# Keys side by side, runs of 32 in the first softmax pass, and other places for TensorE's turns, in a two-layer streaming encoder

## The chip, the cores and the metric

The kernel runs on one core of a Trainium2 chip. The time is the device time of one execution in microseconds, the median of several. The core has TensorE (matrix products; a transposition is also a product, with an identity matrix), VectorE (DVE in the rows), ScalarE (ACT), GpSimd (POOL) and SyncE (SP, which here only issues transfers). Each has an instruction queue of its own, worked off in order; ScalarE also issues transfers (ACTq in the rows). 16 DMA engines move the data.

## The reference

One inference step of an encoder with two layers (DEPTH = 2), width 1024. Two groups of requests share the weights: one prompt of 256 tokens, and 8 decode requests of 16 new tokens, each with a cache of 512 past tokens. A layer is, cut to what matters here:

```python
proj = x @ w_in          # FoX q, k, v, forget gates | Diff q, k, v | gates A, B
# branch A: 8 heads of 64, logits plus a decay summed along the keys
s = einsum('bqhd,bkhd->bhqk', qb, k) * scale + cq - c_k
p = softmax(where(mask, s, -1e30)); oa = einsum('bhqk,bkhd->bqhd', p, v)
# branch B: 4 heads, two softmaxes of 64 wide queries and keys each
s = einsum('bqhcd,bkhcd->bchqk', qb, k) * scale - slopes * dist
p = softmax(where(mask, s, -1e30)); a = p[:, 0] - lam * p[:, 1]
merged = sigmoid(gA) * (oa @ w_ba) + sigmoid(gB) * (ob @ w_bb)
x = LN(ALPHA * x + merged @ w_o)
x = LN(ALPHA * x + (silu(x @ w_g) * (x @ w_u)) @ w_d + sigmoid(x @ w_pg) * (p_ple @ w_pp))
```

The keys and values of a decode request are the cache's 512 and its own 16, 528 in all. Both branches have a cache, so there are 2 x 8 decode streams in a layer and 32 in the run. Outputs are x of both groups and the new keys, values and forget gates.

## The kernel before

All products are made in fp32 quality: a weight tile is split into a high part (`wh`, a cast on ScalarE) and a low part (`wl`, a subtraction on VectorE), an activation likewise (`xh`, `xl`), and three products are summed in PSUM: high times high (L163), low times high (L164), high times low (L165), in `three`. The 384 tokens (256 of the prompt, 128 of the decodes) are three tiles of 128. A weight comes in units of 512 KB (`wr`); a body of a projection runs through eight steps in its input dimension, K tiles of 128, each one call of `three`.

The first half of a layer is one list of such bodies, `work`, for `w_in` and the two branch weights, and the attention is laid between its pieces by hand: `work.fill(us)` emits K tiles until so many (estimated) microseconds are out, then an attention step is emitted, then more K tiles. So the order on each engine is the order in which the program text emits the instructions; nothing reorders them. Smaller steps are handed to a planner: `plan(after, go, pe)` puts a step into a list with a due time on the same estimated clock, and `steps()` runs it between two K tiles when the clock has come to it. A step that holds work for TensorE itself (`pe` true: the transposition of new keys for the output, `out_t`; the decay's sums and turns, `decay_2`, `decay_3`, `sums`; the norm of the prompt's heads; the rows of the per-layer embedding, `ple_rows`) is called a turn here and may stand only behind the first or the third K tile of a body (n = 0 or 2), one to a body.

The attention's decode streams go in a pipeline, one `it` after the other: transposition of the stream's probabilities (`probs`), scores of the next (`scores`), its softmax (`soft`), products of this one with its values (`values`), normalisation of the next (`norm`). Four prompt heads a branch are items of the same kind and stand among its eight streams.

The keys of a stream come as `kr`, [128 partitions, 8, 256]; VectorE transposes them in 32 x 32 blocks into `KT` (L685, two instructions), and GpSimd copies the 16 own keys beside them (L691). A partition of `KT` holds, for each of eight head slices, 8 rows of 34 floats: row c, place r is key 8r + c, and two places in each row take own keys. A score product (L708) takes 264 +- 8 keys of a half `i` in the keys' order, which in `KT` is one float of each row in turn. The 32 score matmuls of a stream are eight tiles of 64 x 32 on the array, twice (d), in the two passes of an fp32 product.

`soft` reads the scores from PSUM: one VectorE instruction for each half of the keys (L717) adds the bias, writes the result to `pm` and keeps the minimum; L720 joins the two minima and ScalarE takes the exponential (L722). For requests 0 to 3 the 16 own keys stand first in `pm`, else last, and the biases (`rt`, `dbs`) are laid out to match.

## Time and profile before

| | |
|---|---|
| median of 3 runs | 1377.43 us (1376.71 to 1377.6) |
| profiled execution | 1381.31 us |
| its span | 1379.5 us |
| granted clock of TensorE, mean | 0.993 |
| TensorE busy | 1329.3 us, 96% |
| VectorE, ScalarE, GpSimd busy | 730.8, 532.2, 173.9 us |
| moved by DMA | 235.12 MB, 170 GB/s |

The span begins with the first instruction and ends with the last, and the profiled execution's time has 1.8 us around it. Busy time is the union of an engine's instructions. TensorE's weight loads (PEld) run beside its products. The lines named are those of the kernel before. The attention of the first layer lies between 87 and 354 us, that of the second between 771 and 981 us.

### The profile page before, as it was taken

How to read it: one execution, taken by the hardware profiler on the slowest of the kernel's cores; microseconds unless marked ns; L12 is line 12 of the kernel's file. 1: busy time of each engine (PE TensorE's matmuls, PEld its weight loads, DVE VectorE, ACT ScalarE, POOL GpSimd, SP SyncE). 2: the span in 40 equal slices, each digit the busy share in tenths (PEclk: the TensorE clock that was granted, in tenths of full speed). 3: DMA queues.
4: the chain of work that ended last, by engine and by line, in shares of the span. 5: the costliest groups of instructions: out<-in, count | busy, mean ns of one | idle time of the engine just before them, and what ended most of it. 6: DMA issues, size and time to landing. Idle time of an engine off the chain costs nothing. (4 is left out here: it accounts for less than half of the span.)

```text
span 1379.5 us, 22688 instructions
## 1 busy us (share of the span) xinstructions
PE 1329.3 (96%) x9102; PEld 1173.8 (85%) x9102; DVE 730.8 (53%) x1290; ACT 532.2 (39%) x1015; POOL 173.9 (13%) x370
## 2 busy tenths in 40 slices
PE   6989999999999999999999999999899999999997
PEld 6978787778889999999998777877788899999996
DVE  3555556656635444444565556666566444344355
ACT  3434544343433333333333335444444333233241
POOL 0042222213200000000014112211132000000001
PEclk9999999999999999999999999999999999999999
DMA  8869897835334344344669697887352444444351
GB/s 249 238 171 266 238 260 204 240 108 193 125 122 123 122 123 138 121 126 153 192 193 255 170 262 241 224 239 211 103 203 89 121 123 130 130 127 131 123 184 46
DMA packets 179673, 235.12 MB, mean 170 GB/s; under 512 B 13392, under 2 KB 143984, under 8 KB 179568
## 3 DMA queue, kind: packets, MB, share of 16 engines
q1 hardware_dynamic: 136272, 190.65, 46.7%
q10 hardware_dynamic: 43296, 43.03, 11.0%
q8 instruction: 71, 1.16, 0.4%
q14 instruction: 34, 0.28, 0.1%
HBM read 223.90 MB, written 9.75 MB: 169 GB/s over the span
## 5 line engine op out<-in xcount | busy, mean ns | idle before, releaser
L163 PE MATMUL tp<-xh,wh 128*128 128x384 f32 x1216 | 419.8, 345 | 0.0
L165 PE MATMUL tp<-xh,wl 128*128 128x384 f32 x1216 | 410.7, 338 | 0.6 <-DVE wl L362 0.6
L164 PE MATMUL tp<-xl,wh 128*128 128x384 f32 x1216 | 408.6, 336 | 0.0
L145 DVE TENSOR_TENSOR wl<-wr,wh 128x1024 fp32r<-128x1024 f32 x158 | 196.2, 1242 | 236.8 <-ACT wh L144 236.5
L144 ACT CAST wh<-wr 128x1024 fp32r<-128x1024 f32 x162 | 170.0, 1049 | 251.8 <-PE zz L165 137.6
L163 PEld LDWEIGHTS tp<-xh,wh 128*128 128x128 f32 x1216 | 228.5, 188 | 8.9 <-issue 7.1
L164 PEld LDWEIGHTS tp<-xl,wh 128*128 128x128 f32 x1216 | 229.2, 188 | 0.8
L165 PEld LDWEIGHTS tp<-xh,wl 128*128 128x128 f32 x1216 | 228.0, 188 | 1.5 <-DVE wl L362 1.2
L362 DVE TENSOR_TENSOR wl<-wr,wh 128x1024 fp32r<-128x1024 f32 (+1 forms) x88 | 115.3, 1310 | 54.4 <-ACT wh L359 54.1
L359 ACT CAST wh<-wr 128x1024 fp32r<-128x1024 f32 (+1 forms) x88 | 92.5, 1051 | 37.6 <-PE tp L164 15.9
L1088 POOL TENSOR_TENSOR st<-st,mhalf 128x1 f32<-128x1 f32 x8 | 12.2, 1523 | 646.4 <-DVE st L1087 646.4
L163 PE MATMUL zz<-wh,pT 128*128 128x512 f32 x216 | 84.8, 393 | 0.0
L165 PE MATMUL zz<-wh,ev 128*128 128x512 f32 x216 | 84.6, 392 | 0.0
L164 PE MATMUL zz<-wl,pT 128*128 128x512 f32 x216 | 84.4, 391 | 0.0
L685 DVE STREAM_TRANSPOSE KT<-kr 128x1024 f32<-128x1024 f32 x64 | 76.5, 1225 | 0.0
L691 POOL COPY KT<-s 32x32 f32<-32x32 f32 x256 | 70.1, 274 | 12.5 <-POOL zp L731 0.2
L708 PE MATMUL S<-KT,s 64*32 64x272 f32 (+1 forms) x1024 | 70.3, 658 | 0.0
L163 PE MATMUL tp<-wh,xh 128*128 128x256 f32 (+1 forms) x192 | 57.7, 300 | 6.9 <-DVE s L262 3.6
L164 PE MATMUL tp<-wl,xh 128*128 128x256 f32 (+1 forms) x192 | 56.3, 293 | 3.7 <-DVE wl L362 3.7
L165 PE MATMUL tp<-wh,xl 128*128 128x256 f32 (+1 forms) x192 | 55.8, 291 | 0.0
L722 ACT ACTIVATE pm<-pm,nmx 128x528 f32<-128x528 f32 x32 | 23.6, 737 | 76.7 <-DVE nmx L720 76.7
L163 PE MATMUL tp<-s,wh 128*128 128x384 f32 x128 | 46.6, 364 | 3.3 <-DVE s L323 1.8
(230 smaller groups left out, 1919.4 us busy)
## 6 DMA issues: line engine op xcount, KB each, us to landing
wr<-in_w_in ACTq DMA_DIRECT2D x72, 512.0 KB
wr<-in_w_ffn_gate SPq DMA_DIRECT2D x44, 512.0 KB
wr<-in_w_ffn_up SPq DMA_DIRECT2D x44, 512.0 KB
wr<-in_w_ffn_down SPq DMA_DIRECT2D x44, 512.0 KB
vr<-in_cache_fox_v SPq DMA_DIRECT2D x16, 1024.0 KB
vr<-in_cache_diff_v SPq DMA_DIRECT2D x16, 1024.0 KB
kr<-in_cache_fox_k SPq DMA_DIRECT2D x16, 512.0 KB
kr<-in_cache_fox_k SPq DMA_DIRECT2D x32, 256.0 KB
```

What stands on the lines that cost most here:

```text
L144: S.copy(hi, raw)
L145: (eng or V).tensor_tensor(lo, raw, hi.bitcast(F32), ALU.subtract)
L163: T.matmul(ps, lhsT=ah, rhs=bh, start=start, stop=False)
L164: T.matmul(ps, lhsT=ah, rhs=bl, start=False, stop=False)
L165: T.matmul(ps, lhsT=al, rhs=bh, start=False, stop=stop)
L359: S.copy(hi, self.raws[len(self.parts)])
L362: return lambda n=len(self.parts) - 1: V.tensor_tensor(lo, self.raws[n], hi.bitcast(F32), ALU.subtract)
L685: V.transpose(kt[:, 4 * c4:4 * c4 + 4], kr[:, 4 * c4:4 * c4 + 4, :].rearrange("p c (n a) -> p c n a", n=8))
L691: G.tensor_copy(KT[r].rearrange("p (j n) c t -> p j n t c", j=2)[:, :, jj, new:new + 2], own.rearrange("p j (t c) -> p j t c", c=8))
L708: T.matmul(s[32 * g:32 * g + 32, i, 0:n[i]], lhsT=qr[r, 2 * g + d, self.b, :], rhs=KT[r, 2 * g + d, :, k0[i]:k0[i] + n[i] // 8].rearrange( ...
L722: S.activation(pm, pm, AF.Exp, bias=nmx, scale=-1.0, accum_out=self.su)
L1088: G.tensor_tensor(st[:, 7:8], st[:, 6:7], mhalf[:, 0:1], ALU.pow)
```

## The change

The places of keys in `KT` become contiguous: a head slice is a row of 272 floats, the half's 256 cached keys and then the 16 own keys, and a score product reads them one beside the other. To have blocks of 32 in that order the key loads take row 64c + 32i + r of the cache (c of 8, half i, r of 32) instead of eight neighbouring rows to a partition. Scores so come in the order of the halves, (i, c, r); the first pass of the softmax, three VectorE instructions instead of two, writes them back in the order of the keys (c, i, r) in runs of 32, and the own keys at the end. One reduction joins three minima. The biases lose their second layout.

The second part is on turns: `plan` now takes the K tiles of a body behind which a turn may stand, (2,) for nearly all, (0,) for the turns of the input and (2, 6) for the rows of the per-layer embedding, which are also due 1 us sooner. A body may take a second turn behind its seventh K tile. In the turns of the input (`turn_x`) all eight transpositions stand ahead of the two splits, for which `split_g` is divided in two. Lastly the first item's normalisation is emitted after 2.5 of the 4.5 us of K tiles that follow its softmax, not ahead of them.

```diff
@@ -71,7 +71,7 @@
     sm[:, SEQ::NQ] = 0.0
     c["c_scan"] = sm
     slopes = 2.0 ** (-8.0 * np.arange(1, H_B + 1) / H_B)
-    kpos = np.concatenate([PAST + jj, np.arange(PAST), PAST + jj])
+    kpos = np.arange(NK)
     qpos = PAST + q
     ds = -8.0 * slopes[row_block() // 2][:, None] * np.abs(qpos[:, None] - kpos[None, :])
     ds = np.where(kpos[None, :] // CHUNK <= qpos[:, None] // CHUNK, ds, -BIG)
...
@@ -171,10 +171,14 @@
             three(ps, hi[:, k % 4, m * P:(m + 1) * P], lo[:, k % 4, m * P:(m + 1) * P],
                   ah[:, k, :], al[:, k, :], k == 0, k == n - 1)
 
-    def split_g(src, tt, hi_t, lo_t, g, n, t=None):
-        t = tp() if t is None else t
+    def turn_g(src, g, n, t):
         for j in range(n):
             T.transpose(t[:, j * P:(j + 1) * P], src[:, (g + j) * P:(g + j + 1) * P], ident)
+
+    def split_g(src, tt, hi_t, lo_t, g, n, t=None):
+        if t is None:
+            t = tp()
+            turn_g(src, g, n, t)
         tv = t[:, :n * P].rearrange("p (k t) -> p k t", k=n)
         hs = hi_t[:, g:g + n, tt * P:(tt + 1) * P]
         S.copy(hs, tv)
...
@@ -288,7 +292,7 @@
                     (S.copy if j % 2 else V.tensor_copy)(kT[:, j, :], ps[:, :NT])
                     if j == 3:
                         for tt in range(3):
-                            plan(2.5 + 4.0 * tt, out_t(tt), True)
+                            plan(2.5 + 4.0 * tt, out_t(tt), (2,))
                 return go
             return [(cols(w_in, D, col + 256 * i), [fm_body(m, out(2 * i + m)) for m in range(2)]) for i in range(2)]
 
...
@@ -326,7 +330,8 @@
 
         plans, clock, due = [], [0.0], [0]
 
-        def plan(after, go, pe=False):
+        def plan(after, go, pe=()):
+
 
             t = clock[0] + after
             i = len(plans)
...
@@ -383,7 +388,8 @@
                                 due[0] += 1
                             was = u
                             clock[0] += cost
-                            while plans and plans[0][0] <= clock[0] and not (plans[0][2] and (n not in (0, 2) or pe)):
+                            pe = pe and n != 6
+                            while plans and plans[0][0] <= clock[0] and not (plans[0][2] and (n not in plans[0][2] or pe)):
                                 pe = pe or plans[0][2]
                                 plans.pop(0)[1]()
                             yield gi, cost
...
@@ -652,10 +658,10 @@
             if g < 2 * NB:
                 K = caches[g // NB][0][g % NB]
                 kr = raws[g] = at.tile([P, 8, 256], F32, name="kr")
-                nc.sync.dma_start(out=kr[32:96], in_=K[:, 0:256].rearrange("(r c) f -> r c f", c=8))
+                nc.sync.dma_start(out=kr[32:96], in_=K[:, 0:256].rearrange("(c p) f -> p c f", c=8))
                 for i in range(2):
                     nc.sync.dma_start(out=kr[part(i, 1):part(i, 1) + 32],
-                                      in_=K[NHF * i:NHF * (i + 1), 256:512].rearrange("(r c) f -> r c f", c=8))
+                                      in_=K[:, 256:512].rearrange("(c i r) f -> i r c f", c=8, i=2)[i])
 
         def load_v(g):
             if g < 2 * NB:
...
@@ -664,11 +670,10 @@
 
         def load_rt(b):
             if b < NB:
-                old, new = (NQ, 0) if b < 4 else (0, PAST)
                 rt = rts[b] = at.tile([P, NK], F32, name="rt")
-                nc.sync.dma_start(out=rt[:, old:old + PAST],
+                nc.sync.dma_start(out=rt[:, 0:PAST],
                                   in_=raw_ap(r8_d[l], b * 8 * PAST, [[PAST, 8], [0, NQ], [1, PAST]]))
-                G.tensor_copy(rt[:, new:new + NQ], nbm[:, b, :])
+                G.tensor_copy(rt[:, PAST:NK], nbm[:, b, :])
 
         def turn_k(g):
 
...
@@ -676,10 +681,9 @@
                 return lambda: None
             st, b = (fx, df)[g // NB], g % NB
             ib = b // 4
-            old, new = (2, 0) if ib == 0 else (0, 32)
-            KT = KTs[g] = at.tile([P, 8, 8, 34], F32, name="KT", bufs=1)
+            KT = KTs[g] = at.tile([P, 8, NHN], F32, name="KT", bufs=1)
             kr = raws.pop(g)
-            kt = KT[:, :, :, old:old + 32].rearrange("p n c r -> p c n r")
+            kt = KT[:, :, 0:NHF].rearrange("p n (c r) -> p c n r", c=8)
 
             def turn(c4):
                 V.transpose(kt[:, 4 * c4:4 * c4 + 4], kr[:, 4 * c4:4 * c4 + 4, :].rearrange("p c (n a) -> p c n a", n=8))
...
@@ -687,9 +691,8 @@
             turn(0)
             for x, jj in ((x, jj) for x in range(2) for jj in range(4)):
                 r = slice(part(ib, x), part(ib, x) + 32)
-                own = st["kv"][0][32 * jj:32 * jj + 32, 2 * x:2 * x + 2, SEQ + NQ * b:SEQ + NQ * b + NQ]
-                G.tensor_copy(KT[r].rearrange("p (j n) c t -> p j n t c", j=2)[:, :, jj, new:new + 2],
-                              own.rearrange("p j (t c) -> p j t c", c=8))
+                G.tensor_copy(KT[r].rearrange("p (j n) t -> p j n t", j=2)[:, :, jj, NHF:NHN],
+                              st["kv"][0][32 * jj:32 * jj + 32, 2 * x:2 * x + 2, SEQ + NQ * b:SEQ + NQ * b + NQ])
             return lambda: turn(1)
 
         class Stream:
...
@@ -701,23 +704,27 @@
             def scores(self):
                 KT, qr, ib = KTs.pop(self.g), self.st["qr"], self.b // 4
                 s = self.s = sp.tile([P, 2, 512], F32, name="S", bufs=2)
-                n = self.n = [NHN if i == ib else NHF for i in range(2)]
-                k0 = [2 if i != ib and ib == 0 else 0 for i in range(2)]
+                n = [NHN if i == ib else NHF for i in range(2)]
                 for d, i, g in ((d, i, g) for d in range(2) for i in range(2) for g in range(4)):
                     r = slice(64 * i, 64 * i + 64)
                     T.matmul(s[32 * g:32 * g + 32, i, 0:n[i]], lhsT=qr[r, 2 * g + d, self.b, :],
-                             rhs=KT[r, 2 * g + d, :, k0[i]:k0[i] + n[i] // 8].rearrange("p c t -> p t c"), start=d == 0, stop=d == 1, skip_group_check=True)
+                             rhs=KT[r, 2 * g + d, 0:n[i]], start=d == 0, stop=d == 1, skip_group_check=True)
 
             def soft(self):
-                n, bias = self.n, self.bias()
+                bias = self.bias()
                 pm = self.pm = at.tile([P, 768], F32, name="pm")[:, 0:NK]
-                nm = sm.tile([P, 2], F32, name="nm2")
-                for i in range(2):
-                    h = slice(n[0] * i, n[0] * i + n[i])
-                    V.tensor_tensor_reduce(out=pm[:, h], in0=self.s[:, i, 0:n[i]], in1=bias[:, h], scale=-0.125,
-                                           scalar=3e38, op0=ALU.add, op1=ALU.min, accum_out=nm[:, i:i + 1])
+                nm = sm.tile([P, 3], F32, name="nm3")
+
+                def part_of(t, i):
+                    return t[:, 0:PAST].rearrange("p (c i r) -> p i c r", c=8, i=2)[:, i]
+
+                for i in range(3):
+                    src, b, out = ((self.s[:, i, 0:NHF].rearrange("p (c r) -> p c r", c=8), part_of(bias, i), part_of(pm, i))
+                                   if i < 2 else (self.s[:, self.b // 4, NHF:NHN], bias[:, PAST:NK], pm[:, PAST:NK]))
+                    V.tensor_tensor_reduce(out=out, in0=src, in1=b, scale=-0.125, scalar=3e38, op0=ALU.add,
+                                           op1=ALU.min, accum_out=nm[:, i:i + 1])
                 nmx = sm.tile([P, 1], F32, name="nmx")
-                V.tensor_tensor(nmx, nm[:, 0:1], nm[:, 1:2], ALU.min)
+                V.tensor_reduce(nmx, nm, mybir.AxisListType.X, ALU.min)
                 self.su = sm.tile([P, 1], F32, name="su1")
                 S.activation(pm, pm, AF.Exp, bias=nmx, scale=-1.0, accum_out=self.su)
 
...
@@ -727,14 +734,12 @@
                 if self.st is df:
                     V.tensor_tensor(rs, rs, coef, ALU.mult)
                 V.tensor_scalar(self.pm, self.pm, rs, None, ALU.mult)
-                new = 0 if self.b < 4 else PAST
-                G.tensor_copy(zp[:, 112:128], self.pm[:, new:new + NQ])
+                G.tensor_copy(zp[:, 112:128], self.pm[:, PAST:NK])
 
             def probs(self):
-                old = NQ if self.b < 4 else 0
                 t = sp.tile([P, 512], F32, name="pt")
                 for c in range(4):
-                    T.transpose(by_block(t[:, c * P:(c + 1) * P]), self.pm[:, old + P * c:old + P * (c + 1)], ident)
+                    T.transpose(by_block(t[:, c * P:(c + 1) * P]), self.pm[:, P * c:P * (c + 1)], ident)
                 tn = self.s[:, 1, 384:512]
                 T.transpose(by_block(tn), zp[:, 112 - NQ * self.b:240 - NQ * self.b], ident)
                 self.pT = at.tile([P, 512], F32, name="pT")
...
@@ -866,7 +871,7 @@
                 ple_load(0)
                 ple_load(1)
                 for tt in range(3):
-                    plan(2.0 + 2.0 * tt, lambda tt=tt: ple_rows(tt), True)
+                    plan(1.0 + 2.0 * tt, lambda tt=tt: ple_rows(tt), (2, 6))
 
         def ple_rows(tt):
             split_g(ple[tt], tt, ple["t"][:, 0], ple["t"][:, 1], 0, 2)
...
@@ -911,10 +916,12 @@
                 def turn_x(tt):
                     t = sp.tile([P, 2, 512], F32, name="S", bufs=2)
                     for g in range(2):
+                        turn_g(x0[:, tt, :], 4 * g, 4, t[:, g, :])
+                    for g in range(2):
                         split_g(x0[:, tt, :], tt, xh, xl, 4 * g, 4, t[:, g, :])
 
                 for tt in (1, 2):
-                    plan(0.3 + 2.9 * (tt - 1), lambda tt=tt: turn_x(tt), True)
+                    plan(0.3 + 2.9 * (tt - 1), lambda tt=tt: turn_x(tt), (0,))
             for _ in range(2):
                 work.split()
             plan(2.4, work.split)
...
@@ -923,15 +930,15 @@
             diag, causal, comb, compm, dbs = [K_[n] for n in ("diag", "causal", "comb", "comp", "dbs")]
             plan(6.0, lambda: load_k(0))
             plan(9.0, decay_1)
-            plan(10.0, decay_2, True)
+            plan(10.0, decay_2, (2,))
             plan(13.0, lambda: load_v(0))
-            plan(14.0, decay_3, True)
+            plan(14.0, decay_3, (2,))
             plan(17.0, lambda: query_slot(fx))
             plan(22.0, lambda: load_k(1))
             plan(30.0, lambda: load_v(1))
             plan(18.5, log_gates)
             plan(21.0, lambdas)
-            plan(23.5, sums, True)
+            plan(23.5, sums, (2,))
             work.fill(upto=2)
             work.fill(upto=4)
             plan(2.5, lambda: late.append(turn_k(0)))
...
@@ -944,8 +951,9 @@
             work.fill(1.0)
             its[0].scores()
             its[0].soft()
+            work.fill(2.5)
             its[0].norm()
-            work.fill(4.5)
+            work.fill(2.0)
             ends, norms, loads = [], [], []
             for i, it in enumerate(its):
                 nx = its[i + 1] if i + 1 < len(its) else None
```

On TensorE the first key turn, that of `s_156` (the new keys, transposed with `c_ident` into `tp`) among the products of a projection; before:

```order
L163 MATMUL tp<-xh,wh 128x384
L164 MATMUL tp<-xl,wh 128x384
L165 MATMUL tp<-xh,wl 128x384
L277 MATMUL tp<-c_ident,s_156 128x128 x4
L163 MATMUL tp<-xh,wh 128x384
L164 MATMUL tp<-xl,wh 128x384
L165 MATMUL tp<-xh,wl 128x384
L163 MATMUL tp<-xh,wh 128x384
L164 MATMUL tp<-xl,wh 128x384
L165 MATMUL tp<-xh,wl 128x384
```

and now:

```order
L163 MATMUL tp<-xh,wh 128x384
L164 MATMUL tp<-xl,wh 128x384
L165 MATMUL tp<-xh,wl 128x384
L163 MATMUL tp<-xh,wh 128x384
L164 MATMUL tp<-xl,wh 128x384
L165 MATMUL tp<-xh,wl 128x384
L163 MATMUL tp<-xh,wh 128x384
L164 MATMUL tp<-xl,wh 128x384
L165 MATMUL tp<-xh,wl 128x384
L281 MATMUL tp<-c_ident,s_156 128x128 x4
L163 MATMUL tp<-xh,wh 128x384
```

It has moved behind two more K tiles of the same body, six products; the other eleven key turns, and those of the decay and the sums, move by as much.

On VectorE the first normalisation of a layer (`rs` is the reciprocal of the sums `su`, `pm` the probabilities, `s_757` a tile of new values that is copied out of `tp`; the reductions are named ISA); before:

```order
L520 ISA nm 128x1
L551 RECIPROCAL rs_798<-su_785 128x4
L555 TENSOR_SCALAR pm<-pm,rs_798 128x128
L555 TENSOR_SCALAR pm<-pm,rs_798 128x256
L555 TENSOR_SCALAR pm<-pm,rs_798 128x128
L555 TENSOR_SCALAR pm<-pm,rs_798 128x256
L262 COPY s_757<-tp 128x256
L577 COPY pT<-S 128x384
L717 ISA pm,nm_877<-S,rt 128x272
L717 ISA nm_877 128x1
L717 ISA pm,nm_877<-S,rt 128x256
L717 ISA nm_877 128x1
```

and now:

```order
L526 ISA nm 128x1
L266 COPY s_757<-tp 128x256
L557 RECIPROCAL rs_823<-su_785 128x4
L561 TENSOR_SCALAR pm<-pm,rs_823 128x128
L561 TENSOR_SCALAR pm<-pm,rs_823 128x256
L561 TENSOR_SCALAR pm<-pm,rs_823 128x128
L561 TENSOR_SCALAR pm<-pm,rs_823 128x256
L583 COPY pT<-S 128x384
L724 ISA pm,nm_877<-S,rt 128x8x32
L724 ISA nm_877 128x1
L724 ISA pm,nm_877<-S,rt 128x8x32
L724 ISA nm_877 128x1
```

The copy of `s_757` stands ahead of the reciprocal and its four multiplications, and the reductions of a stream's softmax are three, two of 8 x 32 columns and one of 16.

On SyncE, which issues transfers in this order, the loads at the end of the attention (`wr` is a unit of weights, `ev` a tile of the embedding rows `p_prompt` and `p_sample`, `vr` cached values); before:

```order
L663 DMA vr<-in_cache_diff_v 128x4x512 x2
L138 DMA wr<-in_w_branch_diff 128x4x256 x2
L859 DMA ev<-in_p_prompt 128x256
L138 DMA wr<-in_w_branch_diff 128x4x256 x2
L859 DMA ev<-in_p_prompt 128x256
L859 DMA ev<-in_p_sample 128x256
L138 DMA wr<-in_w_out 128x1024 x2
```

and now:

```order
L669 DMA vr<-in_cache_diff_v 128x4x512 x2
L138 DMA wr<-in_w_branch_diff 128x4x256 x3
L864 DMA ev<-in_p_prompt 128x256
L138 DMA wr<-in_w_branch_diff 128x4x256
L864 DMA ev<-in_p_prompt 128x256
L864 DMA ev<-in_p_sample 128x256
L138 DMA wr<-in_w_out 128x1024 x2
```

The first embedding rows go out behind a third unit of `w_branch_diff` instead of behind the second.

## Rows read from the trace of the kernel before

**Rows 1.** The page's first part: busy us and share of each engine.

```profile
PE 1329.3 (96%) x9102; PEld 1173.8 (85%) x9102; DVE 730.8 (53%) x1290; ACT 532.2 (39%) x1015; POOL 173.9 (13%) x370
```

**Rows 2.** Groups by line: instruction, count | busy us, mean ns | idle before.

```profile
L685 DVE STREAM_TRANSPOSE KT<-kr 128x1024 f32<-128x1024 f32 x64 | 76.5, 1225 | 0.0
...
L708 PE MATMUL S<-KT,s 64*32 64x272 f32 x512 | 69.9, 673 | 0.0
...
L754 PE MATMUL o<-vr,pT 128*32 128x128 f32 x1024 | 34.6, 276 | 1.7 <-ACT pT L741 1.7
L754 PEld LDWEIGHTS o<-vr,pT 128*32 128x32 f32 x1024 | 26.0, 109 | 22.3 <-issue 7.7 <-ACT pN L743 6.6 <-ACT wh L359 5.8
...
L520 DVE CUSTOM_DVE_ANT_0 pm<-S,z 128x128 f32<-128x128 f32 x16 | 4.6, 289 | 10.9 <-PE S L538 10.9
```

**Rows 3.** Timeline of the first decode stream: start, length in us, instruction.

```profile
98.06 0.59 ACT L741 COPY pT<-pt 128x512 f32<-128x512 f32 x1 [3.70 <-DVE s L262]
...
98.06 2.17 PE L708 MATMUL S<-KT,s 64*32 64x272 f32 x32
...
98.54 0.17 PEld L708 LDWEIGHTS S<-KT,s 64*32 64x32 f32 x8 [0.30 <-issue]
...
99.03 0.17 PEld L708 LDWEIGHTS S<-KT,s 64*32 64x32 f32 x8 [0.32 <-issue]
...
100.16 1.08 PE L754 MATMUL o<-vr,pT 128*32 128x128 f32 x32
```

**Rows 4.** Timeline of the last decode stream, TensorE alone.

```profile
969.97 2.25 PE L708 MATMUL S<-KT,s 64*32 64x256 f32 x32
972.15 1.08 PE L754 MATMUL o<-vr,pT 128*32 128x128 f32 x32
```

**Rows 5.** Timeline behind a Fox prompt head.

```profile
86.99 2.20 PE L708 MATMUL S<-KT,s 64*32 64x272 f32 x32
...
87.61 0.56 DVE L577 COPY pT<-S 128x384 f32<-128x384 f32 x1 [1.88 <-ACT pT L576]
```

**Rows 6.** Waits of TensorE: us in total, times, longest.

```profile
PE tp L277 <- ACT s L300: 11.7, 12, 1.0
...
PE tp L164 <- DVE wl L362: 3.7, 3, 1.8
PE tp L163 <- DVE s L262: 3.6, 2, 2.2
...
PE S L177 <- DVE xl L181: 2.8, 2, 1.4
PE tp L177 <- ACT s L315: 2.3, 2, 1.2
...
PE tp L448 <- PE tp L165: 0.7, 2, 0.3
PE tp L457 <- DVE lg L264: 0.6, 2, 0.3
```

**Rows 7.** Timeline at one key turn.

```profile
152.19 0.34 PE L165 MATMUL tp<-xh,wl 128*128 128x384 f32 x1
...
152.72 0.34 PE L165 MATMUL tp<-xh,wl 128*128 128x384 f32 x1
...
154.07 0.66 PE L277 MATMUL tp<-c_ident,s 128*128 128x128 f32 x4 [1.00 <-ACT s L300]
```

**Rows 8.** Timeline at the first normalisation.

```profile
84.39 1.01 DVE L555 TENSOR_SCALAR pm<-pm,rs 128x128 f32<-128x128 f32 x4
...
86.24 0.82 PE L560 MATMUL S<-c_ident,pm 128*128 128x128 f32 x6
```

**Rows 9.** Windows: stretch, busy us of each engine, clock, DMA share, GB/s.

```profile
87.00:90.00 3.00, 3.00 (x41) 1.48 (x42) 1.14 (x4) 0.48 (x1) 0.00 (x0) 0.50 0.02 5
98.06:354.00 255.94, 248.15 (x2285) 204.86 (x2285) 154.88 (x351) 114.50 (x287) 54.21 (x147) 0.99 0.76 218
780.00:800.00 20.00, 20.00 (x196) 17.30 (x197) 10.54 (x30) 8.95 (x26) 2.31 (x10) 1.00 1.08 265
```

More of the change, by code (lines that the diff above doesn't have):

```diff
@@ L123, in constants @@
         K_["comp"] = cload("c_comp", [P, 2])
-        K_["dbs"] = cload("c_dbs", [P, NK + NQ])
+        K_["dbs"] = cload("c_dbs", [P, NK])
     mhalf = const.tile([P, 8], F32, name="mhalf")
@@ L778, in bias @@
             def bias(self):
-                return dbs[:, 0:NK] if self.b < 4 else dbs[:, NQ:NK + NQ]
+                return dbs
             def finish(self, todo):
@@ L990, in layer @@
                     plan(0.5, diff_prompt_scale)
-                    plan(4.0, lambda: diff_prompt_norm(0), True)
-                    plan(9.0, lambda: diff_prompt_norm(1), True)
+                    plan(4.0, lambda: diff_prompt_norm(0), (2,))
+                    plan(9.0, lambda: diff_prompt_norm(1), (2,))
                 if nx:
```

## The prediction

> **What bounds the kernel now.** I read the page's busy line first: TensorE works through 96% of the span and no other engine through more than 53% [rows 1]. So a microsecond taken from TensorE's own row of work, or from its idle time, shortens the run, and one taken elsewhere does not, unless TensorE waits for it. Next I read the groups by line, each tile shape apart, for what TensorE does at a rate below its usual one: the scores of the decode streams (L708) and the products with the values (L754) are both 1024 matmuls, in 32 streams of 32, and a score takes 673 ns where a product takes 276 [rows 2]. The timeline of one stream shows the rounds in which these go [rows 3], and the last stream's two rows show the same pace as the first's [rows 4]. Then the waits, for what TensorE stands idle for [rows 6], and last the load on VectorE and on the DMA engines in the attention stage [rows 9], which the change touches too.
>
> The profiled execution took 1381.31 us (span 1379.5 us), 3.9 us above the median of 1377.43. I sum against 1381.31 and take the same 3.9 us off at the end.
>
> **A: keys side by side (-32 us).** Before, one score matmul reads keys that lie 34 floats, 136 bytes, apart. The weight loads of the rounds start at 98.06 (with the first matmul), 98.54 and 99.03, so a round of eight matmuls, which lie on different pieces of the array, takes 0.485 us [rows 3]. With 256 or 272 keys, 264 in the mean, that is 1.84 ns per key; the 32 matmuls of a stream are four rounds, the two passes of the fp32 product counted. The product with the values reads its 128 columns side by side, and its rounds, of four, are as far apart as one weight load is long, 109 ns [rows 2]: 0.85 ns per column. (Eight such rounds make the stream's 1.08 us: 7 x 0.109 + 0.276 = 1.04 [rows 2, 3].) A round of 272 contiguous keys is then 0.231 us, of 256 keys 0.218; I take 0.225. What a matmul takes beyond its round is 276 - 109 = 167 ns for the contiguous one [rows 2]; the score's 673 - 485 = 188 ns is nearly the same, so it is a fixed tail. From the first score to the first product of the stream there are four rounds and one tail: 4 x 0.485 + 0.19 = 2.13 us by this, and 2.10 and 2.18 us by the rows of the first and the last stream [rows 3, 4]. After the change: 4 x 0.225 + 0.17 = 1.07, and I put 0.03 on top for the hand-over, which makes 1.10.
>
> Something else then decides in some streams: the product needs the transposed probabilities. ScalarE's copy of them ends 0.59 us after the first score [rows 3], in good time for 1.10. Where a Fox prompt head stands ahead of the scores, VectorE makes the second of two copies and ends at 88.17, 1.18 us after the first score at 86.99 [rows 5]. There are eight such places, four to a layer; I count 1.23 us for them. The sum: 24 x (2.13 - 1.10) = 24.7 and 8 x (2.13 - 1.23) = 7.2, together 32 us. The bounds: nothing, if the stride isn't what makes the round slow; 39 us, if the tail goes too (32 x (2.13 - 0.90) = 39). I take 32, since the nearest row, the product with the values, has rounds and a tail both.
>
> [...]
>
> What A adds lies on VectorE: three reductions instead of two for a softmax, in runs of 32 keys. The smallest reduction shown, 128 columns, takes 289 ns [rows 2]; the new one has 16 columns, so I bound it between 0 and 289 ns, and the two in runs between no change and twice their 0.44 us, if short runs cost what a stride cost TensorE. VectorE is busy for 154.88 of 255.94 us there [rows 9], 61%, and the next to need the probabilities is the transposition a whole stream later, some 14 us; so 0 on the path, with up to 1 us per stream late in what stands behind it on VectorE, the low halves of the weights (term G). POOL's own-key copies and the bias without its copied columns have no one waiting, as POOL is busy for 54 of 256 us [rows 9].
>
> **B: twelve key turns behind the third K tile (-12.2 us).** At each TensorE waits for ScalarE's copy of the keys, 11.7 us in 12 times [rows 6]. In the timeline the last product of the first K tile starts at 152.72 and the turn at 154.07: 1.35 us, against 0.17 between products inside a tile, so 1.18 us is lost. A K tile takes 0.53 us (152.19 to 152.72) [rows 7]. The order puts two more K tiles, 1.06 us, ahead of each turn, so 0.12 us of the wait is left: 12 x 1.06 = 12.7, less 0.5 for a start that is never as neat: 12.2. Bounds: 9 (where ScalarE's copy itself is late) to 14.
>
> **C: all eight transposes before a split (-3.2 us).** TensorE waits for VectorE's first low half before it may turn the second half, 2.8 us in two times [rows 6]; with the restart of 0.18 each (1.18 - 1.00 in B), 3.2. The splits are then late by the second half's turns, half a microsecond, for a product that stands one or two K tiles on: 0 to +1.
>
> **D: the first normalisation is issued later (-1.6 us).** TensorE waits 3.6 us in two times for a copy on VectorE (L262) that stands behind four multiplications [rows 6]; these run 84.39 to 85.40 [rows 8]. The copy now stands ahead of them, but the transposition of the same probabilities, which went at 86.24 [rows 8], needs their end; it can move up to 85.45 and no further. So 0.8 us per layer, not 1.8.
>
> **E: the small turns of decay and sums (-2.0 us).** 0.7 + 0.6 us in four waits [rows 6], with four restarts of 0.18. Two K tiles cover each.
>
> **F: the turns of the per-layer embedding rows (0).** Now two of three stand behind the last product, with waits of 2.3 us in two times [rows 6] and one behind them for the low half. After, they stand among the products, but SP issues the first row's load behind one more weight load, which may make the first turn wait as long. Bounds -3 to +3; I take 0.
>
> **G: what is late next (+2 us).** TensorE comes to its weights about 1 us sooner in each stream. It already waits 3.7 us in three times for a low half (L362) on VectorE [rows 6]. I let this grow by half, +2; bounds 0 to +16, half of A, which is the second rival.
>
> Sum: -32 - 12.2 - 3.2 - 1.6 - 2.0 + 2 = -49.0. 1381.31 - 49.0 = 1332.3, and against the median 1377.43 - 49.0 = **1328 us**.
>
> **Rivals.**
> *The array sets the pace (1360 us).* If eight matmuls side by side are slow because they share the array's input or the PSUM, contiguous keys change nothing, A is 0 and 17 us of the other terms are left: 1377.4 - 17 = 1360. For it: the score's shape is the only one with a height of 64 and four heads in a row. [...]
>
> *Half of A is handed back (1344 us).* The stream's other engines keep their pace: ScalarE's and VectorE's halves of the weights come late, or the products wait for the probabilities in all streams and not in eight. Then 16 of 32 us return: 1328 + 16 = 1344. For it: VectorE gets longer by up to 1 us a stream. Against it: it is idle in 39% of the stage, and the schedule issues the halves ahead of their use.
>
> *Slower: the loads of the keys (1392 us).* A partition's eight rows of keys now lie 64 rows, 128 KB, apart in memory, where they were neighbours, 2 KB apart. A stream has 512 x 512 floats of keys, 1.05 MB; 16 streams in 255.94 us are 66 GB/s of 218, 30% of the bytes, and of the DMA engines' share of 0.76 that is 0.23 [rows 9]. The densest stretch shows 1.08 [rows 9]; 0.76 + 0.23(f - 1) reaches it where the packets take f = 2.4 times as long, and from there TensorE waits for keys. At f = 2.7 the share would be 1.15, 6.6% above, and over the two layers' 466 us of streams (98 to 354, and 771 to 981) that is +31 us; A is hidden by it, and 17 us remain: 1377.4 + 31 - 17 = 1392. Against it: the packets stay 1 KB, the transposition of keys has never waited for its load (idle 0.0) [rows 2], and the loads of the values already jump as far, 128 rows.
>
> **How the numbers follow.** The forecast has 0.75, half of A handed back 0.14, the array's pace 0.07, the key loads 0.04. The forecast's own range: the terms' good ends (A 39, B 14, F -3, G 0) give 1377.4 - (39 + 14 + 3.2 + 1.6 + 2.0 + 3) = 1315; the bad ends that may come together (B 9, F +3, G +5) give 1328 + 3 + 3 + 3 = 1337. To hold 8 in 10 it takes in the second rival with a margin: 1315 to 1347. A measurement of this kernel can tell 0.2%, 2.8 us, from no change. Forecast and first two rivals are all faster: 0.96; of the key loads' 0.04 a quarter lies near f = 2.4 and about cancels: 0.01 no change; 0.03 slower.
>
> **What would show it.** In the profile after: the scores' rounds 0.23 us apart, and 1.1 us from first score to first product (A; 2.1 means the first rival); no wait of TensorE at the key turns over 0.2 us, as against 1.0 (B); no wait for the low half in the turns of the input (C); the transposition behind the first normalisation at once behind the multiplications (D). Waits of TensorE for the low halves or for the probabilities, summed over 10 us, would show the second rival; idle time of VectorE's key transposition for its load, the third. The prediction is wrong if the sum of these is right and the span is not.

## The result and the profile after

The changed kernel takes 1337.19 us (median of 4 runs, 1335.77 to 1338.52), the kernel before 1377.51 us on the same chip (4 runs): the ratio is 0.9708 with an interval of 0.9691 to 0.9725, so 40.3 us less. The forecast was 1328. A second measurement on another chip, among the experiments, gave 1339.49 against 1378.07, 0.9723 (0.9708 to 0.9738).

The profiled execution of the changed kernel took 1336.69 us, 44.6 less than that of the kernel before (1381.31). In the two traces TensorE's products of the projections, taken in order, stand 22.6 us sooner at the end of the first layer's projections and attention and 44.5 sooner at the end of the second's, and between and behind those stages the difference does not move by more than 0.1 us. So all of it lies where the prediction looked for it.

The page's busy line after, to be held against [rows 1]; TensorE is busy for 34.9 us less, VectorE for 7.2 more:

```profile
PE 1294.4 (97%) x9102; PEld 1169.4 (88%) x9102; DVE 738.0 (55%) x1354; ACT 532.4 (40%) x1015; POOL 161.9 (12%) x370
```

The groups by line, for [rows 2] (L710 are the scores, L759 the products with the values, L689 VectorE's transposition of the keys, L724 the softmax's first pass):

```profile
L689 DVE STREAM_TRANSPOSE KT<-kr 128x1024 f32<-128x1024 f32 x64 | 76.3, 1223 | 0.0
...
L710 PE MATMUL S<-KT,s 64*32 64x272 f32 x512 | 37.4, 409 | 0.0
...
L759 PE MATMUL o<-vr,pT 128*32 128x128 f32 x1024 | 35.3, 280 | 1.1 <-ACT pT L746 1.1
...
L724 DVE CUSTOM_DVE_ANT_1 pm<-S,rt 128x256 f32<-128x256 f32 x32 | 12.3, 422 | 15.0 <-PE S L710 14.5
...
L724 DVE CUSTOM_DVE_ANT_0 pm<-S,rt 128x16 f32<-128x16 f32 x16 | 2.7, 170 | 0.0
```

and of the kernel before the softmax's first pass on 256 columns:

```profile
L717 DVE CUSTOM_DVE_ANT_0 pm<-S,rt 128x256 f32<-128x256 f32 x16 | 6.8, 423 | 10.0 <-PE S L708 10.0
```

A score is down from 673 to 409 ns, and runs of 32 cost VectorE nothing: 422 ns for 256 columns against 423. What VectorE has more of is the third reduction, 170 ns. The first decode stream, for [rows 3], in which the first product follows 1.05 us after the first score instead of 2.10:

```profile
90.74 1.12 PE L710 MATMUL S<-KT,s 64*32 64x272 f32 x32
...
91.79 1.08 PE L759 MATMUL o<-vr,pT 128*32 128x128 f32 x32
```

TensorE's waits (us in total, times, longest), for [rows 6]. The key turns, the input's second half and the decay are gone from the list; the low halves, the new L499 and L795 have grown:

```profile
PE tp L165 <- DVE wl L367: 5.2, 5, 2.3
...
PE tp L164 <- DVE wl L367: 3.9, 3, 1.6
PE S L795 <- ACT osb L762: 3.2, 2, 1.6
PE tp L163 <- DVE s L499: 3.1, 1, 3.1
PE tp L176 <- DMA ev<-in_p_prompt: 2.8, 2, 1.4
...
PE S L566 <- DVE pm L561: 0.8, 2, 0.6
...
PE tp L163 <- DVE s L266: 0.7, 1, 0.7
```

Where these come from is in three places of the timeline. At 47 us, in the first layer alone, ScalarE's cast stands 4.22 us for a weight to land; VectorE's subtraction stands behind the cast, its copy of the sums' turn behind the subtraction, and TensorE, which needs that PSUM tile, behind the copy:

```profile
44.28 1.04 ACT L364 CAST wh<-wr 128x1024 fp32r<-128x1024 f32 x1 [4.22 <-DMA wr<-in_w_in]
...
45.35 1.22 DVE L367 TENSOR_TENSOR wl<-wr,wh 128x1024 fp32r<-128x1024 f32 x1 [4.42 <-ACT wh L364]
...
46.50 0.54 DVE L499 COPY s<-tp 8x384 f32<-8x384 f32 x1
...
47.09 0.45 PE L163 MATMUL tp<-xh,wh 128*128 128x384 f32 x1 [3.09 <-DVE s L499]
```

In each layer, behind a key turn, two subtractions take 3.87 us together where one takes 1.2, while GpSimd copies the Diff queries (L307), and the scores that come after the wait last 2.04 us instead of 1.12 (this is the first layer; in the second, at 799 us, 3.99 and 1.78):

```profile
142.59 1.89 POOL L307 COPY s<-s 32x2048 f32<-32x2048 f32 x1
...
142.82 3.87 DVE L367 TENSOR_TENSOR wl<-wr,wh 128x1024 fp32r<-128x1024 f32 x2 [0.61 <-ACT wh L364]
...
145.62 0.44 PE L165 MATMUL tp<-xh,wl 128*128 128x384 f32 x1 [2.15 <-DVE wl L367]
...
146.53 2.04 PE L710 MATMUL S<-KT,s 64*32 64x256 f32 x32
```

The windows (stretch, busy time of each engine, granted clock, DMA share, GB/s) show the granted clock behind both waits: 0.50 and 0.51 (second and third row). From 90.74 to 92.00, where the scores take 1.12 us, it is 1.00. The first row is the wait at 47 us itself, with the DMA engines at a share of 1.03.

```profile
43.00:47.50 4.50, 1.41 (x8) 1.09 (x7) 2.11 (x3) 1.04 (x1) 0.00 (x0) 1.00 1.03 266
47.66:51.07 3.41, 3.41 (x13) 3.41 (x12) 1.17 (x3) 0.50 (x1) 0.00 (x0) 0.50 0.74 176
146.60:150.00 3.40, 3.40 (x62) 2.13 (x65) 1.12 (x8) 1.02 (x3) 0.00 (x0) 0.51 0.47 93
```

The third place, once a layer, gives back a whole stream's gain. GpSimd takes 2.48 us for the prompt heads' norm, VectorE's eight multiplications stand behind it, the softmax, ScalarE and its copy L762 behind those. None of that got shorter (2.47, 1.66 and 0.24 us before for the norm, the multiplications and the copy, at 291.26, 293.76 and 297.09), so TensorE, 1.05 us sooner, waits 1.59 us at the end instead of 0.43 (by the trace; no run below changes this place):

```profile
270.62 1.15 PE L710 MATMUL S<-KT,s 64*32 64x256 f32 x32
270.67 2.48 POOL L639 TENSOR_TENSOR rst<-ssq,mhalf 128x8 f32<-128x8 f32 x1 [0.38 <-DVE ssq L637]
...
273.19 1.66 DVE L856 TENSOR_SCALAR s<-s,rst 128x128 f32<-128x128 f32 x8 [1.54 <-POOL rst L639]
...
276.59 0.24 ACT L762 COPY osb<-o 128x128 f32<-128x128 f32 x1
...
276.89 0.43 PE L795 MATMUL S<-osb,c_comb 128*64 128x128 f32 x2 [1.59 <-ACT osb L762]
```

### The profile page after: what moved, and what is told of

It reads as the page before. It is cut to its first block, busy times and chain, and to the rows that moved or that the text cites. A ratio compares the mean times of both kernels' runs of the same rounds, so it can differ in the third digit from the quotient of the medians.

```text
span 1334.9 us, 22737 instructions
## 1 busy us (share of the span) xinstructions
PE 1294.4 (97%) x9102; PEld 1169.4 (88%) x9102; DVE 738.0 (55%) x1354; ACT 532.4 (40%) x1015; POOL 161.9 (12%) x370
## 4 chain that ended last, share of the span: by engine, by line
PE 86%; DVE 6%; DMA 4%; issue 3%; ACT 2%; POOL 0%; DVEq 0%; SPq 0%; POOLq 0%; ACTq 0%
PE tp L163 18%; PE tp L165 17%; PE tp L164 17%; PE zz L163 8%; PE zz L165 8%; PE zz L164 8%; PE S L710 2%; PE o L759 2%; DMA wr<-in_w_in 2%; DVE wl L367 2%; DVE KT L689 1%; PE pt L742 1%; PE S L544 1%; PE tp L176 1%; DVE pm L724 1%
## 5 line engine op out<-in xcount | busy, mean ns | idle before, releaser
L165 PE MATMUL tp<-xh,wl 128*128 128x384 f32 x1216 | 411.8, 339 | 5.2 <-DVE wl L367 5.2
L165 PEld LDWEIGHTS tp<-xh,wl 128*128 128x128 f32 x1216 | 228.6, 188 | 6.9 <-DVE wl L367 6.9
L367 DVE TENSOR_TENSOR wl<-wr,wh 128x1024 fp32r<-128x1024 f32 (+1 forms) x88 | 118.8, 1352 | 47.2 <-ACT wh L364 46.5
L1096 POOL TENSOR_TENSOR st<-st,mhalf 128x1 f32<-128x1 f32 x8 | 12.2, 1521 | 645.0 <-DVE st L1095 645.0
L165 PE MATMUL zz<-wh,ev 128*128 128x512 f32 x216 | 84.6, 392 | 0.0
L689 DVE STREAM_TRANSPOSE KT<-kr 128x1024 f32<-128x1024 f32 x64 | 76.3, 1223 | 0.0
L694 POOL COPY KT<-s 32x32 f32<-32x32 f32 x256 | 55.2, 216 | 12.5 <-POOL zp L737 0.2
L165 PE MATMUL tp<-wh,xl 128*128 128x256 f32 (+1 forms) x192 | 54.9, 286 | 0.0
L165 PEld LDWEIGHTS zz<-wh,ev 128*128 128x128 f32 x216 | 40.5, 187 | 9.4
L164 PEld LDWEIGHTS zz<-wl,pT 128*128 128x128 f32 x216 | 40.5, 188 | 8.3
```

Source lines behind the costliest of these rows:

```text
L164: T.matmul(ps, lhsT=ah, rhs=bl, start=False, stop=False)
L165: T.matmul(ps, lhsT=al, rhs=bh, start=False, stop=stop)
L367: return lambda n=len(self.parts) - 1: V.tensor_tensor(lo, self.raws[n], hi.bitcast(F32), ALU.subtract)
L689: V.transpose(kt[:, 4 * c4:4 * c4 + 4], kr[:, 4 * c4:4 * c4 + 4, :].rearrange("p c (n a) -> p c n a", n=8))
L694: G.tensor_copy(KT[r].rearrange("p (j n) t -> p j n t", j=2)[:, :, jj, NHF:NHN], st["kv"][0][32 * jj:32 * jj + 32, 2 * x:2 * x + 2, SEQ + ...
```

## The experiments

All times stand beside the kernel before on the same chip: 1378.76 us for the two halves, the input's turns and the later loads; 1378.07 for the changed kernel again, GpSimd's copy, the other place for the order and both waits gone; 1378.01 for the two steps and the last run.

**The two halves of the change, each alone.** The edits are the diff's own pieces: the keys' tile, loads, softmax and biases on the one hand, `plan` and its positions, `turn_x` and the moved normalisation on the other.

> The kernel before with the keys side by side and the softmax in runs of 32, without any of the turns' moves. Theory (the scores gain 1.05 us in each of 32 streams, and this stands by itself): 1377.5 - 33.6 + about 2 of new waits = 1346 us, range 1343 to 1349; first score to first product 1.05 to 1.10 us. Rival (A needs the turns' moves, since TensorE runs into the same waits sooner): half of it comes back at the key turns and the low halves of the weights, 1360 us.

Measured: 1349.26 us, ratio 0.9790 (0.9775 to 0.9805), 29.5 less. The theory held in kind, 3 us short of its 1346 and just outside its range. The low halves' waits (L165) rise from 0.6 to 3.1 us, and L789 (the one at 1.59 us above) from 0.8 to 3.2, with no turn moved:

```profile
PE S L789 <- ACT osb L756: 3.2, 2, 1.6
PE tp L165 <- DVE wl L362: 3.1, 4, 1.4
```

> The kernel before with all of the turns' moves and the later normalisation, keys as before. Theory (what the turns gain is partly taken back by waits that were not there before: the load of a weight at 47 us and the low halves at the second key turn of the Diff branch): measured total of 40.3 less 33.6 of the keys leaves 7 to 10 us, 1368 to 1370 us, with a wait of TensorE near 47 us of 2 to 4 us. Rival (the turns give the full 19 us that were worked out, and it is the keys that hand something back): 1358 to 1360 us.

Measured: 1362.05 us, ratio 0.9882 (0.9864 to 0.9899), 16.7 less. My theory was wrong: the turns alone give nearly all of what was worked out for them, and there is no long wait near 47 us. The two halves sum to 46.2 us, the whole change to 40.3; the missing 6, known to about 4 by the three intervals, appear only with both. The wait at 47 us is a part of them. With the turns alone the load of the weight that is late there goes out at 36.91 us, ahead of the second stream's keys at 37.55; with both changes (the changed kernel run again) it goes out behind them, at 36.62 after 35.59.

**The input's turns.** In `turn_x`, the split again between the two halves' transpositions:

```diff
                     for g in range(2):
                         turn_g(x0[:, tt, :], 4 * g, 4, t[:, g, :])
-                    for g in range(2):
                         split_g(x0[:, tt, :], tt, xh, xl, 4 * g, 4, t[:, g, :])
```

> The changed kernel with the turns of the input as before (each half's four transpositions followed by its split). Theory (a weight lands at about 43 us whatever TensorE does sooner, so what is gained in the first 40 us is waited for there): within 1 us of the changed kernel, 1337 us, the wait at 47 us smaller by about 3 us. Rival (gains in the input stand): 3.2 us slower, 1340.4 us, the wait at 47 us unchanged.

Measured: 1340.12 us, ratio 0.9721 (0.9706 to 0.9736), beside 0.9708 and 0.9723 for the changed kernel: no difference that can be told, and the rival's 3.2 us, 0.0023 in the ratio, can't be excluded either. The 2.8 us of waits in the input are back, and the wait at 47 us is down to 0.21 us, as the theory says; but its reason does not hold in the trace. The weight does not land at the same time whatever TensorE does: its load goes out at 40.83 us instead of 36.62, its cast starts 2.59 us later, and TensorE goes on 2.59 us later. First the changed kernel run again, then this run:

```profile
44.03 1.05 ACT L364 CAST wh<-wr 128x1024 fp32r<-128x1024 f32 x1 [2.96 <-DMA wr<-in_w_in]
...
46.85 0.44 PE L163 MATMUL tp<-xh,wh 128*128 128x384 f32 x1 [1.84 <-DVE s L499]
```

```profile
46.62 1.05 ACT L364 CAST wh<-wr 128x1024 fp32r<-128x1024 f32 x1 [1.34 <-DMA wr<-in_w_in]
...
49.44 0.44 PE L163 MATMUL tp<-xh,wh 128*128 128x384 f32 x1 [0.21 <-DVE s L499]
```

So at this place most of part C's 3.2 us still stands in these two traces. What it is worth in the end is not shown.

**The loads that compete with that weight.** Due times on the planner's clock:

```diff
-            plan(13.0, lambda: load_v(0))
+            plan(33.0, lambda: load_v(0))
-            plan(22.0, lambda: load_k(1))
+            plan(38.0, lambda: load_k(1))
-            plan(30.0, lambda: load_v(1))
+            plan(46.0, lambda: load_v(1))
```

> The changed kernel with the first cached values and the second stream's keys and values loaded later (due at 33, 38 and 46 instead of 13, 22 and 30). Theory (these loads of 1 MB each share the DMA engines with the weights in the first 47 us and make the ninth unit late): the wait of 3.1 us at 47 us falls below 1 us, the half clock behind it goes, 1332 to 1334 us. Rival (the weight is late since its load is issued late, at 35.6 us, when its buffer comes free): the wait stays at 3 us and the time at 1337 us.

Measured: 1336.03 us, ratio 0.9679 (0.9662 to 0.9696), 42.7 less. The wait at 47 us is gone from the list, and in the window from 20 to 47 us the DMA engines are at 0.77 and TensorE is busy throughout; in the changed kernel, run again, they are at 0.95 and TensorE loses 1.84 us. First this run, then the changed kernel again:

```profile
20.00:47.00 27.00, 27.00 (x188) 26.87 (x187) 15.97 (x38) 10.51 (x15) 0.00 (x0) 1.00 0.77 220
780.00:823.00 43.00, 38.47 (x416) 33.12 (x415) 23.69 (x59) 23.14 (x67) 8.88 (x22) 1.00 1.04 260
```

```profile
20.00:47.00 27.00, 25.16 (x176) 24.70 (x176) 14.33 (x35) 10.55 (x15) 0.00 (x0) 1.00 0.95 274
```

So the weight was late because other loads shared the engines with it, and not because its own load was issued late: that goes out at 36.67 us here and at 36.62 in the changed kernel run again, and its cast starts at 41.02 instead of 44.03. The time won is less sure than the wait, and 1336 is nearer to the rival's 1337 than to the theory's 1332 to 1334: a new wait of 3.9 us stands at 823 us, behind ScalarE, which waits for a weight there, in a stretch with the DMA engines at 1.04 (the second row).

**The changed kernel again.**

> The changed kernel once more, on the same chip as the three that follow, and to see whether its new wait at 47 us (3.1 us, VectorE behind a weight that is loaded late) is in every execution or chance. If it is the change's own: again 2 to 4 us there, 1336 to 1338 us against 1377.5 to 1379 before. If chance: gone, 1332 to 1335 us.

Measured: 1339.49 us, ratio 0.9723 (0.9708 to 0.9738). The wait at 47 us is there again, 1.84 us, so it is the change's own and not chance, though wait and time both lie just outside what was expected. Its size varies with the start. In the first profiled execution TensorE had waited 1.64 us for the first weight of the run, here 2.96: there it came 1.0 us sooner to the place at 47 us (44.00 and 45.01) and waited 1.25 us longer, and it went on at nearly the same time (47.09 and 46.85).

**GpSimd's copy.**

```diff
-                    G.tensor_copy(st["qr"][part(1, hh):part(1, hh) + 32], st["qr"][part(0, hh):part(0, hh) + 32])
+                    copy = lambda: G.tensor_copy(st["qr"][part(1, hh):part(1, hh) + 32], st["qr"][part(0, hh):part(0, hh) + 32])
+                    if st is df:
+                        plan(9.0, copy)
+                    else:
+                        copy()
```

> The changed kernel with GpSimd's copy of the Diff queries (32x2048) due 9 us later. Theory (that copy slows VectorE's subtraction beside it from 1.23 to 2.64 us; TensorE then waits 2.2 us for the low half, and its clock falls to half behind the wait, in which the scores take 2.0 instead of 1.05 us): the wait falls to about 0.7 us in each layer, no half clock there, 4 to 6 us faster than the changed kernel. Rival (the subtraction is long for another reason, or the copy slows another one that is waited for): wait still 2 us or more, time within 1 us.

Measured: 1333.73 us, ratio 0.9666 (0.9646 to 0.9685), 5.8 us faster than the changed kernel on the same chip, the intervals apart. At the same place the two subtractions now take 2.36 us for both, the wait is 0.65 us, and the scores take 1.15 us, as at 270.62 us in the changed kernel, where the granted clock is 1.00:

```profile
144.12 2.36 DVE L371 TENSOR_TENSOR wl<-wr,wh 128x1024 fp32r<-128x1024 f32 x2 [0.63 <-ACT wh L368]
...
145.40 0.45 PE L165 MATMUL tp<-xh,wl 128*128 128x384 f32 x1 [0.65 <-DVE wl L371]
...
146.32 1.15 PE L714 MATMUL S<-KT,s 64*32 64x256 f32 x32
```

That the copy slowed the subtraction is shown by this pair of traces: in the changed kernel it takes 2.74 us beside the copy and the next one, without it, 1.21; here, with the copy at 152.86, the two take 2.36 together. So is what the wait did to TensorE's clock: behind 2.15 us the granted clock is 0.51 and the scores take 2.04 us, behind 0.65 they take 1.15. Which of the two is slowed goes, in these traces, with which starts first. In the changed kernel the copy starts first (142.59, subtraction 142.82) and takes 1.89 us, as it does in this run at 152.86, with no subtraction beside it; in the second layer of the run with later loads the subtraction starts first, at 798.45, the copy at 798.50 takes 2.92 us, and TensorE waits only 0.64 us.

**Another place for the keys' order.** Key loads as before, VectorE's transposition writes at a step of 8 floats, the softmax takes the keys in one piece:

```diff
-            kt = KT[:, :, 0:NHF].rearrange("p n (c r) -> p c n r", c=8)
+            kt = KT[:, :, 0:NHF].rearrange("p n (r c) -> p c n r", c=8)
```

> The changed kernel with the key loads as before (eight neighbouring rows to a partition) and the order restored by VectorE's transposition, which writes at a step of 8 floats; the softmax's first pass goes through the keys in one piece. Scores still read contiguous keys. Theory (what counts is only TensorE's reading side by side; 32 keys in a run cost VectorE nothing in the softmax, 422 against 423 ns): if a write at a step costs VectorE as little, within 1.5 us of the changed kernel. Rival (a step of 32 bytes slows the transposition as a step of 136 bytes slowed TensorE's reading, from 1.22 to 2.4 us or more, twice a stream): 5 to 15 us slower than the changed kernel, with more waits for the low halves (L367).

Measured: 1363.40 us, ratio 0.9901 (0.9883 to 0.9918): 24 us slower than the changed kernel, more than the rival allowed. The transposition takes 2168 instead of 1223 ns, and VectorE, with 58 us more of it, makes TensorE wait at the low halves (16.8 us in two rows of the list) and the scores for their keys:

```profile
L689 DVE STREAM_TRANSPOSE KT<-kr 128x1024 f32<-128x1024 f32 x64 | 134.3, 2168 | 0.0
```

**The step alone.** The scores read every second, then every fourth float of the keys' tile.

```diff
-                             rhs=KT[r, 2 * g + d, 0:n[i]], start=d == 0, stop=d == 1, skip_group_check=True)
+                             rhs=KT[r].rearrange("p n t -> p (n t)")[:, NHN * min(2 * g + d, 6):NHN * min(2 * g + d, 6) + 2 * n[i]].rearrange("p (t a) -> p t a", a=2)[:, :, 0], start=d == 0, stop=d == 1, skip_group_check=True)
```

> The changed kernel with the score products reading every second float of the keys' tile (8 bytes apart; so the scores are not those of the keys, and GpSimd clears the unused places once a stream). It measures the pace of a round alone. Theory (the pace falls where a step leaves fewer than two keys in 16 bytes): as side by side, 0.23 us a round and 1.05 to 1.10 us from first score to first product. Rival (any step slows the reading): 0.45 to 0.49 us a round and 2.1 us.

> As the one before, but every fourth float (16 bytes apart). Theory (one key in 16 bytes is one too few): as with 136 bytes, 0.485 us a round, 2.1 us from first score to first product. Rival (only steps of 128 bytes or more are slow): 0.23 us and 1.1 us.

Measured, one stream of each. Step 2: the first product 1.09 us after the first score (93.74 to 94.83).

```profile
93.74 1.16 PE L711 MATMUL S<-KT,s 64*32 64x272 f32 x32
94.83 0.42 PE L760 MATMUL o<-vr,pT 128*32 128x128 f32 x8
```

Step 4: 2.04 us (92.52 to 94.56), rounds 0.46 us apart.

```profile
92.52 2.10 PE L711 MATMUL S<-KT,s 64*32 64x272 f32 x32
...
92.99 0.15 PEld L711 LDWEIGHTS S<-KT,s 64*32 64x32 f32 x8 [0.29 <-issue]
...
93.44 0.18 PEld L711 LDWEIGHTS S<-KT,s 64*32 64x32 f32 x8 [0.30 <-issue]
94.56 0.65 PE L760 MATMUL o<-vr,pT 128*32 128x128 f32 x16
```

So a step of 8 bytes costs 4% (1.09 against 1.05 us) and one of 16 bytes as much as one of 136 (2.04 against 2.10). Both theories came true: of the steps measured the pace holds at 8 bytes and falls at 16. What sets that bound, no run shows.

**Both waits gone.** The query copy and the cache loads of the two edits above together; then the same with the loads later in the first layer alone.

> The changed kernel with the Diff query copy due 9 us later and the first cached values and the second stream's keys and values loaded later, so both new waits are aimed at. If both theories hold: the wait at 47 us under 1 us and those at the second Diff key turns about 0.7 us, 1328 to 1331 us, 6 to 9 us faster than the changed kernel. If only the copy matters: 1331 to 1334 us. If neither: 1336 to 1338 us.

Measured: 1332.72 us, ratio 0.9672 (0.9656 to 0.9687). Both waits are as expected in the trace, and the profiled execution was the shortest of those profiled, 1330.55, but the median is that of the query copy alone: "if only the copy matters".

> The changed kernel with the Diff query copy 9 us later in both layers, and the cached values and second keys loaded later in the first layer alone. In the run with both layers' loads later, TensorE waited 2.0 us (3.9 us in the run with the loads alone) at 817 to 823 us behind ScalarE, which stood at a weight's load. If those later loads caused it: that wait is gone, and 2 to 4 us are won on that run, 1328 to 1331 us. If the wait is chance: 1332 to 1334 us.

Measured: 1333.85 us, ratio 0.9666 (0.9643 to 0.9688). The wait is still there, and longer:

```profile
814.03 1.05 ACT L368 CAST wh<-wr 128x1024 fp32r<-128x1024 f32 x1 [2.83 <-DMA wr<-in_w_in]
...
819.01 0.48 ACT L586 COPY pT<-S 128x384 f32<-128x384 f32 x1 [3.42 <-DMA wr<-in_w_in]
...
819.54 1.72 PE L595 MATMUL o<-pT,s 128*64 128x128 f32 x10 [4.15 <-ACT pT L586]
```

So the later loads of the second layer did not cause it. Those of the first layer are not excluded: the three kernels whose trace has the wait share them, and the query copy alone, without them, does not show it. TensorE also comes to that stretch sooner in the three (the product behind the second Diff key turn starts at 799.73, 795.45 and 796.14 us, with the query copy alone at 800.61), and the DMA engines' share is high there (1.04 in the row of the later loads, where [rows 9] has 1.08 as the most before). And the execution profiled here was the slowest of its five, 1337.52 us, the fastest 1328.87, so the wait may stand in some executions only. Which of these it is, no run settles. The three kernels with the query copy later are faster than the changed kernel with intervals apart; for the later loads alone the intervals touch. The query copy alone is the smallest edit and as fast as any.

## Why the prediction was right, and where it missed 9 us

The direction, the range and the main term were right. Point by point, by the two profiled executions:

- **A** was forecast at 32 us. From the first score to what follows it the 32 streams took 68.1 us before and 35.7 after: 32.4. Its working was not right all through. At the eight places behind a Fox prompt head I had put a bound of 1.23 us by VectorE's copy; the trace has 1.05 to 1.09, since the first products need ScalarE's part only: here they start at 136.38, before VectorE's copy ends at 136.48 (scores, copy and products behind such a head, for [rows 5]):

```profile
135.30 1.15 PE L710 MATMUL S<-KT,s 64*32 64x256 f32 x32
...
135.92 0.56 DVE L583 COPY pT<-S 128x384 f32<-128x384 f32 x1 [0.47 <-ACT pT L582]
...
136.38 0.87 PE L591 MATMUL o<-pT,s 128*64 128x128 f32 x10
```

Against that, two scores at half clock take 1.97 and 1.72. The rival "the array sets the pace" is out by the runs at steps of 2 and 4 floats: the same tiles on the array, and 1.09 and 2.04 us. The scores at half clock before, in the last section, speak against it too. That the tail stays, 32 and not 39 us, was an estimate from the products with the values; what makes the tail, no run shows.
- **B** (12.2), **C** (3.2) and **E** (2.0) came as waits that are no longer in the list. D: 3.6 us before, 0.8 + 0.7 after, so 2.1 instead of 1.6. **F** (0): the turns of the embedding rows and what stands by them wait 2.8 us for the load as foreseen, 4.8 us in all against 3.8 before. A turn that no term had counted, that of the prompt heads' norm, waited 0.9 us before and does not now.
- **G**, what is late next, is the term that was mis-sized: +2 forecast. The waits for the low halves grew by 4.8 us (from 3.7 + 0.6 to 5.2 + 3.9), the weight at 47 us cost 3.1, L795 2.4: 10.3 us of new waits. The clock at half behind two of these places is no net loss against before: that trace has four such stretches besides the one at its end (near 88, 320, 774 and 1000 us), the trace after three (48, 148 and 804), and the mean granted clock is 0.993 before and 0.995 after. I had sized it from the waits of the trace before, by half again. It should have been sized by what stands beside each place once TensorE comes sooner: in the trace before a low half already took 2.50 us beside GpSimd's copy, only no one waited for it:

```profile
155.24 2.86 POOL L303 COPY s<-s 32x2048 f32<-32x2048 f32 x1
...
156.68 2.50 DVE L362 TENSOR_TENSOR wl<-wr,wh 128x1024 fp32r<-128x1024 f32 x1 [0.33 <-ACT wh L359]
```

- **The base.** I took 3.9 us between the profiled execution and the median to stay. Profile to profile the change gives 44.6 us, by the medians 40.3. The profiled execution of before is above 1381; of 31 other executions of that kernel two are. So of the 9 us that are missing 4.3 lie in the base and 4.4 in the terms. By the waits above A to E come to 51.9 us, and 10.3 taken off leave 41.6 of the 44.6. Of the other 3, 1.4 are the wait for the first weight of the run (3.02 us before, 1.64 after), which is chance, as the changed kernel's second trace with 2.96 shows, and which the wait at 47 us took back; the rest is not assigned.

The second rival, half of A handed back, is what happened in part: 6 us by the sum of the two halves alone. By the sign given for it, waits for the low halves or the probabilities of over 10 us, it is just met (5.2 + 3.9 + 1.1 = 10.2), but 6.0 of these stood in the trace before (3.7 + 0.6 + 1.7), so the sign was too weak to tell. The third, slower key loads, did not happen: the transposition of keys still waits for nothing, with loads that jump 128 KB from row to row (the prediction's sum for this rival gives 1391, not 1392).

## What to carry to other kernels

Look at the step, in bytes, of every operand that TensorE streams: 8 bytes between fp32 elements cost 4% here, 16 and 136 bytes doubled the time; put the permutation where runs stay long (the softmax's first pass, free here), and not into a transposition's write (24 us here). When TensorE gets faster in one place, go along the trace and ask at each later place what it stood beside but didn't wait for: slow neighbours that no one waited for became the next waits here (a GpSimd copy beside a VectorE subtraction, 2.74 us instead of 1.21, and prefetches beside a weight load, for which ScalarE stood 4.22 us), and due times that were tuned for the old pace are then the cheap edit.

## What the runs showed that I had not expected

- The scores' old pace did not depend on TensorE's clock (2.20 us at a granted clock of 0.50 [rows 5, 9], 2.17 us at 1.00, the granted clock from 98.06 to 100.20 [rows 3]), the new one does: 2.04 us for the row at 0.51, 1.12 to 1.15 at 1.00. So at half clock little is left of the gain (1.97 and 1.72 us from first score to first product), and a short wait can cost more than its length: behind the one of 2.15 us the scores took 0.9 us longer than the 1.15 they take at 1.00.
- A wait of 2.15 us was followed by a stretch at half clock (0.51 from 146.60 to 150.00), one of 0.65 us at the same place by scores of 1.15 us; at 47 us one of 3.09 us was followed by half clock (0.50 from 47.66 to 51.07), one of 1.84 us, in the changed kernel run again, was not (1.00 in the same stretch).
- VectorE's 32 x 32 transposition takes 1.8 times as long (2168 against 1223 ns) when its writes step 32 bytes.
